# The last chunks of a down-projection, written by hand in a half and two quarters of the tokens

## The chip, the core and the metric

The kernel runs on one core of a Trainium2 chip. The core has a matrix engine (TensorE, PE in the profile, with its weight loads as a row of their own, PEld), a vector engine (DVE), a scalar engine (ACT), a general engine (POOL) and a queue that issues transfers (SP). Each engine works through its own instructions in order and waits on semaphores for the others. The metric is the device time of one execution in microseconds (us); lower is better.

## The reference, cut to what matters

A trunk of two layers over 512 tokens of 1024 channels, all in float32. Only the end of the second layer and the final normalization bear on the change:

```
def swiglu(h, w_gate, w_up, w_down):
    g = jnp.einsum("bsd,df->bsf", h, w_gate)
    u = jnp.einsum("bsd,df->bsf", h, w_up)
    return jnp.einsum("bsf,fd->bsd", jax.nn.silu(g) * u, w_down)
...
        x = x + swiglu(h, w_gate[l], w_up[l], w_down[l])
    return rmsnorm(x, final_norm_g)
```

The final normalization of a token needs the sum of the squares of all its 1024 channels, and so every product of the down-projection for that token. Tokens do not need one another here.

## The kernel before, in words

Activations are kept with channels on the 128 partitions and the 512 tokens along the free dimension: `x[0]` to `x[7]` are eight tiles of 128 channels by 512 tokens. A weight block is 128 by 128. To keep float32 precision each operand is split into a high and a low part in TensorE's float32r type, and a block costs three products: high by high, high by low and low by high (lines 844 to 846 for the stretch in question, 186 to 188 elsewhere). Each product loads its own weights. The low parts of the weights are made by DVE (line 144) from a copy by ACT (line 135), five pairs ahead of their use.

The last down-projection of the second layer is `last_down`. The SwiGLU values come in two halves of 11 blocks of 128 hidden channels; this function handles the second half. For two of the eight output chunks it runs all 11 blocks at once, for the other six only the first 7; this leaves for those six chunks the last 4 blocks (`KL = 4`), whose weights it has put aside in `last`. So the end of the kernel is six chunks of 4 blocks of three products: 72 products over all tokens. They are run once for tokens 0 to 255 and once for tokens 256 to 511, so 144 products of 256 columns.

After each chunk's 12 products, DVE adds the result to `x` (line 848), ACT squares the sum (line 850), and DVE adds the square to a running sum `run` (line 852). After the six chunks of a half, `scale_of` does the normalization: four products of one column each (line 303; float32, so each stands twice in a trace) sum the squares over the partitions, a chain of nine small DVE steps (`rsqrt`, lines 285 to 293) takes the inverse root, two DVE steps build a diagonal matrix (line 315, tile `dg`), and a product (line 330, tile `rbc`) spreads the result over the partitions. Then each chunk of the half, already multiplied by its channel gain on ACT (line 862, tile `fo`), is multiplied by `rbc` on DVE (line 866) or by a copy `rf` of it on POOL (line 864), and pairs of chunks are sent to memory, 256 KB each, four transfers a half (line 868).

What sets the order of all this before the change is a scheduler that reorders instructions within each engine by its own estimate of times. It has laid the first half's normalization under the second half's products, and two of the last products ahead of the end of the 7-block part.

Of the kernel before, what the change touches and what calls it, by code (L numbers as in the profile page):

```python
# [19 lines left out]
F32 = mybir.dt.float32  # L20
F32R = mybir.dt.float32r
I32 = mybir.dt.int32
AF = mybir.ActivationFunctionType
# [5 lines left out]
S = 512  # L29
L = 2  # L30
P = 128
KC = D // P
FF = 2816
FC = FF // P
FH = FC // 2
# [3 lines left out]
RMS_EPS = 1e-6  # L39
# [3 lines left out]
RQ = 0.375 * -0.5  # L43
UNITS = 96
KL = 4
FIN_POOL = [[0, 1, 2, 3, 4], [0, 1]]


C_MIXG, C_FFNG, C_SC, C_GLUB, C_DW, C_DWB, C_LNG, C_LNB, C_SUB = 0, 8, 16, 22, 26, 88, 90, 92, 94
# [29 lines left out]
def trunk(ctx, tc, xT, pos, wu, cv, lamv, cst, out):  # L79
    nc = tc.nc  # L80
    V, A, G, T = nc.vector, nc.scalar, nc.gpsimd, nc.tensor

    def pool(name, bufs, **kw):
        return ctx.enter_context(tc.tile_pool(name=name, bufs=bufs, **kw))
    cp = pool("cp", 1)
    pw = pool("pw", 6)
    ph = pool("ph", 8)
# [15 lines left out]
    x = [cp.tile([P, S], F32, name=f"x{k}") for k in range(KC)]  # L103
# [79 lines left out]
    def mm3(ps, rh, first, last, w=None):  # L183

        hi, lo = w or block()
        T.matmul(ps, lhsT=hi, rhs=rh[:, 0, :], start=first, stop=False)  # L186
        T.matmul(ps, lhsT=hi, rhs=rh[:, 1, :], start=False, stop=False)  # L187
        T.matmul(ps, lhsT=lo, rhs=rh[:, 0, :], start=False, stop=last)  # L188
# [86 lines left out]
        (V if (k == KC - 1 if last is None else last) else eng).tensor_add(run, run, sq)  # L275
        return run

    def rsqrt(a, n, key):

        y = sm.tile([P, n], F32, tag=f"rq{key}", name=f"rq{key}", bufs=2)
        t = sm.tile([P, n], F32, tag=f"rt{key}", name=f"rt{key}", bufs=2)
        a2 = sm.tile([P, n], F32, tag=f"ra{key}", name=f"ra{key}", bufs=2)
        V.tensor_scalar(y.bitcast(I32), a.bitcast(I32), -0.5, 1597463007.0, ALU.mult, ALU.add)
        V.tensor_scalar(a2, a, 0.375 ** 2, None, ALU.mult)
        V.tensor_mul(t, a, y)
        V.tensor_mul(t, t, y)
        V.scalar_tensor_tensor(t, t, -10.0 / 3.0, t, ALU.add, ALU.mult)
        V.scalar_tensor_tensor(y, t, 5.0, y, ALU.add, ALU.mult)  # L290
        V.tensor_mul(t, a2, y)
        V.tensor_mul(t, t, y)
        V.scalar_tensor_tensor(y, t, -3.0, y, ALU.add, ALU.mult)
        return y

    def scale_of(parts, mul, eps, key, pool, ptag, n=4):

        ps = pool.tile([P, n], F32, tag=ptag, name="ssps")  # L300
        for b in range(n):
            for i, t in enumerate(parts):
                T.matmul(ps[:, b:b + 1], lhsT=t[:, b * P:b * P + P], rhs=consts["ones_d"][:, 0:1],
                         start=i == 0, stop=i == len(parts) - 1)
        a = sm.tile([P, n], F32, tag="sca" + key, name="sca", bufs=2)
        V.tensor_scalar(a, ps, mul, eps, ALU.mult, ALU.add)
        y = rsqrt(a, n, key)
# [155 lines left out]
    class Pair:  # L463
# [349 lines left out]
    def last_down(acts):  # L813

        NA = KC - 6
        H = S // 2
        run = pt.tile([P, S], F32, tag="t", name="run")
        for dc in range(KC):  # L820
            n = FH if dc < NA else FH - KL
            ps = acc.tile([P, S], F32, tag="acc", name="od")
            for k in range(n):
                mm3(ps, acts[k], k == 0, k == n - 1)
            V.tensor_add(x[dc], x[dc], ps)
            if dc == 0:
# [6 lines left out]
        outs = [ph.tile([P, 2, S], F32, tag="h", name=f"fo{i}") for i in range(KC // 2)]  # L833
        g = [cvt[:, C_FING + k:C_FING + k + 1] for k in range(KC)]
        rb = []
        for i in range(2):
            cs = slice(i * H, i * H + H)
            for j in range(6):
                p, tag = ((acc, "acc"), (sc, "sc"))[j % 2]
                q = p.tile([P, H], F32, tag=tag, name="ol")  # L840
                for k in range(KL):
                    hi, lo = last[j][k]
                    rh = acts[FH - KL + k]
                    T.matmul(q, lhsT=hi, rhs=rh[:, 0, cs], start=k == 0, stop=False)
                    T.matmul(q, lhsT=hi, rhs=rh[:, 1, cs], start=False, stop=False)
                    T.matmul(q, lhsT=lo, rhs=rh[:, 0, cs], start=False, stop=k == KL - 1)
                t = x[NA + j][:, cs]
                V.tensor_add(t, t, q)
                sq = pe.tile([P, H], F32, tag="e", name="sqh")
                A.activation(sq, t, AF.Square)  # L850
                if j < 5:
                    V.tensor_add(run[:, cs], run[:, cs], sq)
            st = scale_of([run[:, cs], sq], 1.0, RMS_EPS, f"f{i}", tp, "tp", n=2)
            next(st)
            rb.append(next(st))
        for i in range(2):
            cs = slice(i * H, i * H + H)
            r = pt.tile([P, H], F32, tag="t", name="rf")
            A.copy(r, rb[i])
            for k in range(KC):  # L860
                o = outs[k // 2][:, k % 2, cs]
                A.activation(o, x[k][:, cs], AF.Copy, scale=g[k])
                if k in FIN_POOL[i]:
                    G.tensor_mul(o, o, r)
                else:
                    V.tensor_mul(o, o, rb[i])
                if k % 2:
                    nc.sync.dma_start(out[k - 1:k + 1, :, cs].rearrange("k p t -> p k t"), outs[k // 2][:, :, cs])

    def lambdas():  # L870

# [21 lines left out]
    run = None  # L893
    h = []
    state = {}
    for l in range(L):
        cb = l * C_LAYER
        st = {"run": None, "h": [None] * KC}
# [22 lines left out]
        for half in range(2):  # L921
            acts = []
            for f in range(FH):
                if r is None:
                    mr = make_r(run2)
                    next(mr)
                    r = next(mr)
# [4 lines left out]
                t = pt.tile([P, S], F32, tag="t", name="tg")  # L932
# [3 lines left out]
                a = (py if f < 8 else pv).tile([P, 2, S], F32R, tag=("yb", "ya", "v")[f // 4], name="act")  # L936
# [8 lines left out]
        h = st["h"]  # L945
        run = st["run"]
# [109 lines left out]
```

## Time and profile before

| what | value |
| --- | --- |
| median of 3 runs | 1180.51 us (1180.06 to 1187.22) |
| profiled execution | 1177.73 us |
| its span, first to last instruction | 1176.0 us |
| TensorE busy | 1139.2 us, 97% of the span |
| VectorE busy | 642.5 us, 55% |
| mean granted TensorE clock | 0.986 of full speed |

The profiled execution is a run of its own, 2.8 us under the median of the timed ones. Times within it, such as "at 1161.23", are us from the start of its span. In the rows further down, L846 is line 846 of the kernel, `out<-in` are the program's names for tiles, and `xN` counts instructions. The granted clock is 1.00 at 2.4 GHz and 0.50 at 1.2 GHz.

### The profile page before, as it was taken

To read this page: it belongs to the slowest core of one execution; us is meant where nothing else is said; L and a number is where in the kernel's file an instruction comes from. 1 tells how busy PE (TensorE), PEld (TensorE's weight loads), DVE (VectorE), ACT (ScalarE), POOL (GpSimd) and SP (SyncE) were. 2 spreads that over 40 slices of the span, in tenths; PEclk is the share of its full clock that TensorE was granted. 3 is DMA by queue.
4 is the path that set the end of the run, shared out by engine and by line. 5 is a ranking of instruction groups with operands and counts; after the bars stand their busy time and mean duration, and the time that the engine had idled before them with its cause. 6 is when DMAs were issued, how large, how long until landed. Compare 5 with 4: busy or idle time off the path is not lost.

```text
span 1176.0 us, 14329 instructions
## 1 busy us (share of the span) xinstructions
PE 1139.2 (97%) x5238; PEld 944.2 (80%) x5238; DVE 642.5 (55%) x1152; ACT 497.6 (42%) x1023; POOL 187.5 (16%) x217
## 2 busy tenths in 40 slices
PE   7989899999999999999999999999999999999995
PEld 5878787888888888888888787788888888888885
DVE  6687785564443344444436988746544333444345
ACT  6636566643332233333345466665333222333323
POOL 1421212311110010110123212122101000011001
PEclk9999899999999999999999999999999999999998
DMA  5895834432322223232247866453232322323212
GB/s 196 218 219 123 198 85 111 106 125 90 108 90 99 98 91 107 90 102 95 91 130 182 199 147 152 114 134 118 93 104 90 107 91 95 103 90 108 90 55 72
DMA packets 48614, 138.53 MB, mean 118 GB/s; under 512 B 6912, under 2 KB 9216, under 8 KB 48544
## 3 DMA queue, kind: packets, MB, share of 16 engines
q1 hardware_dynamic: 29888, 88.79, 23.5%
q0 software_dynamic: 18656, 48.83, 17.6%
q8 instruction: 41, 0.67, 0.2%
q14 instruction: 29, 0.24, 0.1%
HBM read 122.79 MB, written 2.23 MB: 106 GB/s over the span
## 4 chain that ended last, share of the span: by engine, by line
PE 83%; DVE 6%; DMA 3%; issue 3%; ACT 3%; SPq 1%; POOL 0%; DVEq 0%; ACTq 0%; POOLq 0%
PE od L186 8%; PE od L187 8%; PE od L188 8%; PE gp L188 7%; PE gp L187 7%; PE up L188 7%; PE up L187 7%; PE up L186 7%; PE gp L186 7%; PE qk L186 3%; PE qk L187 2%; PE qk L188 2%; DMA w<-wu 1%; DVE acc L576 1%; PE cc L187 1%
## 5 line engine op out<-in xcount | busy, mean ns | idle before, releaser
L135 ACT CAST w<-raw 128x512 fp32r<-128x512 f32 x384 | 237.6, 622 | 491.8 <-PE od L188 147.1
L144 DVE TENSOR_TENSOR w<-raw,w 128x512 fp32r<-128x512 f32 x265 | 186.8, 706 | 247.2 <-ACT w L135 246.6
L935 POOL TENSOR_TENSOR tg<-tg,r 128x512 f32<-128x512 f32 x44 | 57.7, 1313 | 520.6 <-ACT tg L934 511.0
L187 PE MATMUL gp<-h,w 128*128 128x512 f32 x352 | 137.3, 390 | 0.3 <-DVE h L265 0.3
L188 PE MATMUL gp<-h,w 128*128 128x512 f32 x352 | 137.3, 390 | 0.0
L186 PE MATMUL up<-h,w 128*128 128x512 f32 x352 | 137.2, 390 | 0.0
L186 PE MATMUL gp<-h,w 128*128 128x512 f32 x352 | 137.2, 390 | 0.0
L188 PE MATMUL up<-h,w 128*128 128x512 f32 x352 | 137.1, 390 | 0.0
L187 PE MATMUL up<-h,w 128*128 128x512 f32 x352 | 137.1, 390 | 0.0
L187 PE MATMUL od<-act,w 128*128 128x512 f32 x328 | 127.8, 390 | 0.0
L186 PE MATMUL od<-act,w 128*128 128x512 f32 x328 | 127.8, 389 | 0.0
L188 PE MATMUL od<-act,w 128*128 128x512 f32 x328 | 127.7, 389 | 0.0
L138 POOL DMA_DIRECT2D w<-wu x70 | 60.7, 871 | 282.5 <-ACT w L137 236.8
L576 DVE SCALAR_TENSOR_TENSOR acc<-pad,cvt,acc 128x511 f32<-128x511 f32 (+14 forms) x120 | 88.1, 734 | 2.7
L187 PEld LDWEIGHTS gp<-h,w 128*128 128x128 f32 x352 | 66.1, 188 | 14.5 <-DVE h L265 0.7
L186 PEld LDWEIGHTS up<-h,w 128*128 128x128 f32 x352 | 66.1, 188 | 14.0 <-DVE x L901 0.4
L186 PEld LDWEIGHTS gp<-h,w 128*128 128x128 f32 x352 | 66.1, 188 | 13.8 <-ACT h L264 0.2
L187 PEld LDWEIGHTS up<-h,w 128*128 128x128 f32 x352 | 66.1, 188 | 13.7
L188 PEld LDWEIGHTS up<-h,w 128*128 128x128 f32 x352 | 66.1, 188 | 13.6
L188 PEld LDWEIGHTS gp<-h,w 128*128 128x128 f32 x352 | 66.1, 188 | 13.5
L186 PEld LDWEIGHTS od<-act,w 128*128 128x128 f32 x328 | 61.6, 188 | 12.8
L187 PEld LDWEIGHTS od<-act,w 128*128 128x128 f32 x328 | 61.6, 188 | 12.7
(254 smaller groups left out, 1988.6 us busy)
## 6 DMA issues: line engine op xcount, KB each, us to landing
raw<-wu SPq DMA_DIRECT2D x135, 512.0 KB, 3.4
raw<-wu POOLq DMA_DIRECT2D x56, 512.0 KB, 6.3
w<-wu POOLq DMA_DIRECT2D x70, 256.0 KB, 4.7
pk<-hl SPq DMA_DIRECT2D x64, 128.0 KB, 6.9
pq<-hl SPq DMA_DIRECT2D x64, 64.0 KB, 5.0
x<-xT SPq DMA_DIRECT2D x8, 256.0 KB, 8.2
yT<-fo SPq DMA_DIRECT2D x8, 256.0 KB, 2.2
raw<-wu SPq DMA_DIRECT2D x2, 256.0 KB, 6.7
```

The source lines that it names most:

```text
L135: A.copy(t[:, 0, :], raw)
L138: G.dma_start(t[:, 1, :], wu[u, :, 4 * P * half:4 * P * half + 4 * P], accum_op=ALU.add)
L144: sub()
L186: T.matmul(ps, lhsT=hi, rhs=rh[:, 0, :], start=first, stop=False)
L187: T.matmul(ps, lhsT=hi, rhs=rh[:, 1, :], start=False, stop=False)
L188: T.matmul(ps, lhsT=lo, rhs=rh[:, 0, :], start=False, stop=last)
L576: V.scalar_tensor_tensor(a[:, d:], pad[:, :S - d], cvt[:, c - d:c - d + 1], a[:, d:], ALU.mult, ALU.add)
L935: G.tensor_mul(t, t, r)
```

## The change

The six chunks are run in three parts instead of two: tokens 0 to 255, 256 to 383 and 384 to 511, so 72 products of 256 columns and 144 of 128 columns. The whole end is taken out of the scheduler's hands (`tc.manual_schedule()`), so it stands in each engine's queue as it is written. The sums and the inverse root of a part are written under the next part's products: its sums after the next part's second chunk, the small DVE steps of its root between that part's additions (`between`). Chunks 2 and 3 of the six, and 5 and 6, get the two banks of one PSUM buffer. A chunk pair of the first half is now multiplied in one POOL instruction (512 columns), four of them, and the quarters by DVE, four chunks in one instruction. The multiplications and transfers of both quarters stand at the very end. The output still leaves in eight transfers of 256 KB, but those of the quarters are made of rows of 128 tokens, 512 bytes each, where a half has rows of 1024 bytes.

```
-    def rsqrt(a, n, key):
+    def rsqrt(a, n, key, between=lambda: None):
...
         V.tensor_mul(t, a, y)
+        between()
         V.tensor_mul(t, t, y)
         V.scalar_tensor_tensor(t, t, -10.0 / 3.0, t, ALU.add, ALU.mult)
+        between()
         V.scalar_tensor_tensor(y, t, 5.0, y, ALU.add, ALU.mult)
         V.tensor_mul(t, a2, y)
+        between()
...
+        with tc.manual_schedule():
+            finale(acts, last, run)
+
+    def finale(acts, last, run):
+        NA = KC - 6
+        H = S // 2
+        parts = [slice(0, H), slice(H, H + P), slice(H + P, S)]
...
+        def between(n=1):
+            while todo and n:
+                todo.pop(0)()
+                n -= 1
+
+        def product(j, i):
+            cs = parts[i]
+            n = cs.stop - cs.start
+            if j % 3 == 0:
+                q = acc.tile([P, n], F32, tag="acc", name="ol")
+            else:
+                if j % 3 == 1:
+                    two.append(sc.tile([P, 2, S], F32, tag="sc", name="ol"))
+                q = two[-1][:, j % 3 - 1, :n]
+            for k in range(KL):
+                hi, lo = last[j][k]
+                rh = acts[FH - KL + k]
+                T.matmul(q, lhsT=hi, rhs=rh[:, 0, cs], start=k == 0, stop=False)
+                T.matmul(q, lhsT=hi, rhs=rh[:, 1, cs], start=False, stop=False)
+                T.matmul(q, lhsT=lo, rhs=rh[:, 0, cs], start=False, stop=k == KL - 1)
+            return q
...
+        def step(j, i, sqs):
+            q = product(j, i)
+            cs = parts[i]
+
+            def added():
                 t = x[NA + j][:, cs]
                 V.tensor_add(t, t, q)
+                sq = pe.tile([P, cs.stop - cs.start], F32, tag="e", name="sqh")
                 A.activation(sq, t, AF.Square)
+                sqs[j] = sq
+                if i:
+                    scaled(NA + j, i - 1)
                 if j < 5:
+                    todo.insert(0, lambda: V.tensor_add(run[:, cs], run[:, cs], sq))
+            todo.append(added)
+
+        def wide(o, dst, r, eng):
+            eng.tensor_mul(o, o, r.unsqueeze(1).to_broadcast(list(o.shape)))
+            nc.sync.dma_start(dst.rearrange("k p t -> p k t"), o)
...
+        for j in range(6):
+            step(j, 0, sqs[0])
+            between(2)
+        between(9)
...
+        for i, pool, tag in ((1, tp, "tp"), (2, av, "av")):
+            for j in range(2):
+                step(j, i, sqs[i])
+                between(2)
+            st = scale(i - 1, pool, tag)
+            for j in range(2, 6):
+                step(j, i, sqs[i])
             next(st)
+            between(99)
+            rb = next(st)
+            rbs.append(rb)
+            if i == 1:
+                r = pt.tile([P, H], F32, tag="t", name="rf")
+                A.copy(r, rb)
+                for k in range(4):
+                    leave(k, r, G)
+        st = scale(2, tp, "tp")
+        for j in range(6):
+            scaled(NA + j, 2)
+        next(st)
+        rb = next(st)
+        leave4(0, 1, rbs[1])
+        leave4(4, 1, rbs[1])
+        leave4(0, 2, rb)
+        leave4(4, 2, rb)
```

Up to the end of the 7-block part every engine's queue holds the same work in the same order as before, but for the two early products and the gain multiplications of the two finished chunks. In the rows below `w_8866`, `w_8883`, `w_8900`, `w_8915`, `w_8932` and `w_8948` are the weights of chunks 1 to 6, `x_103` to `x_108` the six tiles of `x`, and the names in brackets are the engines that an instruction waits for.

TensorE, in the second part, where the sums of the first half (`ssps`) stand. Before, second half's chunks 2 and 3:

```order
L846 MATMUL ol<-act,w_8883 128x256
L303 MATMUL ssps<-ones_d,run 128x1 [waits DVE_49,Pool_49]
L844 MATMUL ol<-act,w_8883 128x256
L845 MATMUL ol<-act,w_8883 128x256
L846 MATMUL ol<-act,w_8883 128x256
L844 MATMUL ol<-act,w_8900 128x256
L845 MATMUL ol<-act,w_8900 128x256
```

Now, first quarter's chunks 2 and 3:

```order
L875 MATMUL ol<-act,w_8883 128x128
L301 MATMUL ssps<-ones_d,run 128x1 [waits DVE_49,Pool_49]
L301 MATMUL ssps<-ones_d,sqh 128x1 [waits Activation_49]
L301 MATMUL ssps<-ones_d,run 128x1
L301 MATMUL ssps<-ones_d,sqh 128x1
L873 MATMUL ol<-act,w_8900 128x128 [waits DVE_49]
L874 MATMUL ol<-act,w_8900 128x128
```

The sums stand in one block, the products around them have 128 columns in place of 256, and chunk 3 begins with a wait for DVE.

TensorE, in the first half, from chunk 2 to the next chunk. Before (the scheduler ran chunk 4 next):

```order
L844 MATMUL ol<-act,w_8883 128x256
L845 MATMUL ol<-act,w_8883 128x256
L846 MATMUL ol<-act,w_8883 128x256
L844 MATMUL ol<-act,w_8915 128x256 [waits Activation_49]
L845 MATMUL ol<-act,w_8915 128x256
```

Now:

```order
L873 MATMUL ol<-act,w_8883 128x256
L874 MATMUL ol<-act,w_8883 128x256
L875 MATMUL ol<-act,w_8883 128x256
L873 MATMUL ol<-act,w_8900 128x256 [waits DVE_49,Activation_49]
L874 MATMUL ol<-act,w_8900 128x256
```

Chunk 3 writes the second bank of the buffer that chunk 2 has just filled, and its wait on DVE runs up to the addition that reads chunk 2. The same stands between chunks 5 and 6.

DVE, from the end of the last products on. Before:

```order
L848 TENSOR_TENSOR x_107<-x_107,ol 128x256 [waits PE_49]
L852 TENSOR_TENSOR run<-run,sqh 128x256 [waits Activation_49]
L848 TENSOR_TENSOR x_108<-x_108,ol 128x256 [waits PE_49]
L866 TENSOR_TENSOR fo_8953<-fo_8953,rbc 128x256 [waits Activation_49]
L866 TENSOR_TENSOR fo_8954<-fo_8954,rbc 128x256 x2
L306 TENSOR_SCALAR sca<-ssps 128x2 [waits PE_49]
```

Now:

```order
L889 TENSOR_TENSOR x_107<-x_107,ol 128x128 [waits PE_49]
L896 TENSOR_TENSOR run<-run,sqh 128x128 [waits Activation_49]
L889 TENSOR_TENSOR x_108<-x_108,ol 128x128
L313 TENSOR_SCALAR sca<-ssps 128x1 [waits PE_49]
...
L322 TENSOR_SCALAR dg<-idr,sca 128x128 [waits DVE_49]
L900 TENSOR_TENSOR fp_8957<-fp_8957,rbc 128x512
L900 TENSOR_TENSOR fp_8957<-fp_8957,rbc 128x512 [waits Activation_49]
L900 TENSOR_TENSOR fp_8958<-fp_8958,rbc 128x512 [waits PE_49,Activation_49]
L900 TENSOR_TENSOR fp_8958<-fp_8958,rbc 128x512 [waits Activation_49]
```

The three multiplications ahead of the root are gone, the addition of chunk 6 has no wait of its own (that of chunk 5 now waits for the last product of both), and four wide multiplications close the queue.

## Rows read from the trace of the kernel before

**Rows 1.** The page: its span, and busy time of each engine.
```profile
span 1176.0 us, 14329 instructions
PE 1139.2 (97%) x5238; PEld 944.2 (80%) x5238; DVE 642.5 (55%) x1152; ACT 497.6 (42%) x1023; POOL 187.5 (16%) x217
```

**Rows 2.** Chain of waits, last 15 us: start, length, what.
```profile
1161.39 0.12 PE ol L846
...
1162.39 1.09 DVE fo L866 x3
...
1163.53 1.07 PE ssps L303 x8
...
1164.81 0.42 DVE rqf L285
...
1165.30 0.61 DVE rtf L287
...
1167.32 0.49 DVE dg L315 x2
...
1167.94 1.21 PE rbc L330 x2
...
1170.00 0.33 DVEq L1052
1170.33 1.32 DVE fo L866 x4
```

**Rows 3.** Timeline of TensorE, first and last of the 256-column products: start, length, what.
```profile
1143.20 0.39 PE L188 MATMUL od<-act,w 128*128 128x512 f32 x1
...
1143.43 0.28 PE L846 MATMUL ol<-act,w 128*128 128x256 f32 x1
...
1161.23 0.28 PE L846 MATMUL ol<-act,w 128*128 128x256 f32 x1
```

**Rows 4.** The same view around 30 us: products of one column.
```profile
29.79 1.02 PE L303 MATMUL ssps<-ones_d,run 128*128 128x1 f32 x8 [2.46 <-issue]
30.67 0.47 PE L186 MATMUL cc<-h,w 128*128 128x512 f32 x1
```

**Rows 5.** The same view at 84 us: products of 128 columns.
```profile
84.31 0.41 PE L483 MATMUL ps<-maskr,idr 128*128 128x128 f32 x1
84.53 0.41 PE L481 MATMUL ps<-pk,pq 128*128 128x128 f32 x1
```

**Rows 6.** Groups by line and shape: busy us, mean ns | idle before.
```profile
L844 PE MATMUL ol<-act,w 128*128 128x256 f32 x47 | 13.4, 287 | 0.0
...
L848 DVE TENSOR_TENSOR x<-x,ol 128x256 f32<-128x256 f32 x12 | 5.1, 421 | 2.9 <-PE ol L846 2.6
...
L315 DVE TENSOR_SCALAR dg<-idr,sca 128x128 f32<-128x128 f32 x4 | 1.0, 285 | 0.1
...
L525 ACT ACTIVATE junk<-o 128x128 bf16<-128x128 f32 x32 | 8.9, 277 | 6.4 <-PE o L523 6.4
...
L933 DVE TENSOR_TENSOR tg<-gp,r 128x512 f32<-128x512 f32 x44 | 30.2, 691 | 52.5 <-PE gp L188 52.5
...
L935 POOL TENSOR_TENSOR tg<-tg,r 128x512 f32<-128x512 f32 x44 | 57.7, 1313 | 520.6 <-ACT tg L934 511.0
```

**Rows 7.** Stretches: length, busy of PE, PEld, DVE, ACT, POOL, clock, DMA, GB/s.
```profile
27.00:30.60 3.60, 1.14 (x10) 0.84 (x8) 2.56 (x4) 1.96 (x4) 2.53 (x6) 1.00 0.72 202
30.60:34.00 3.40, 3.40 (x17) 2.81 (x18) 2.81 (x18) 0.77 (x3) 1.63 (x4) 1.00 0.95 213
80.30:83.70 3.40, 1.14 (x5) 0.57 (x4) 3.26 (x5) 2.22 (x5) 0.78 (x1) 1.00 1.09 265
83.70:87.10 3.40, 3.27 (x11) 2.89 (x12) 3.29 (x6) 1.23 (x3) 0.62 (x2) 0.51 1.06 275
```

**Rows 8.** DMA queue, 27.15 to 28.35, then 1169.5 to 1175.5: packets, MB, share of 16.
```profile
q1 hardware_dynamic: 160, 0.07, 26.1%
...
q1 hardware_dynamic: 1088, 1.05, 52.1%
```

More of the change, by code (lines that the diff above doesn't have):

```diff
@@ L45 @@
 KL = 4
-FIN_POOL = [[0, 1, 2, 3, 4], [0, 1]]
 C_MIXG, C_FFNG, C_SC, C_GLUB, C_DW, C_DWB, C_LNG, C_LNB, C_SUB = 0, 8, 16, 22, 26, 88, 90, 92, 94
@@ L294, in rsqrt, with sums @@
         return y
-    def scale_of(parts, mul, eps, key, pool, ptag, n=4):
-        ps = pool.tile([P, n], F32, tag=ptag, name="ssps")
+    def sums(ps, parts, n):
         for b in range(n):
@@ L304, in scale_of @@
                          start=i == 0, stop=i == len(parts) - 1)
+    def scale_of(parts, mul, eps, key, pool, ptag, n=4, between=lambda: None):
+        ps = parts
+        if isinstance(parts, list):
+            ps = pool.tile([P, n], F32, tag=ptag, name="ssps")
+            sums(ps, parts, n)
         a = sm.tile([P, n], F32, tag="sca" + key, name="sca", bufs=2)
         V.tensor_scalar(a, ps, mul, eps, ALU.mult, ALU.add)
-        y = rsqrt(a, n, key)
+        y = rsqrt(a, n, key, between)
         def diag(p, v, dt, tag, eng, **kw):
@@ L832, in last_down @@
         last = [[block() for _ in range(KL)] for _ in range(6)]
-        outs = [ph.tile([P, 2, S], F32, tag="h", name=f"fo{i}") for i in range(KC // 2)]
-        g = [cvt[:, C_FING + k:C_FING + k + 1] for k in range(KC)]
[L835 to L846, printed above, removed]
+        with tc.manual_schedule():
+            finale(acts, last, run)
@@ new lines, in finale, with scaled @@
+    def finale(acts, last, run):
+        NA = KC - 6
+        H = S // 2
+        parts = [slice(0, H), slice(H, H + P), slice(H + P, S)]
+        g = [cvt[:, C_FING + k:C_FING + k + 1] for k in range(KC)]
+        half = [ph.tile([P, 2, H], F32, tag="h", name=f"fo{i}") for i in range(KC // 2)]
+        quarter = [ph.tile([P, KC, P], F32, tag="h", name=f"fp{i}") for i in range(2)]
+        todo = []
+        two = []
+        def between(n=1):
[18 more added lines that the diff above has]
+            return q
+        def scaled(k, i):
+            o = quarter[i - 1][:, k, :] if i else half[k // 2][:, k % 2, :]
+            A.activation(o, x[k][:, parts[i]], AF.Copy, scale=g[k])
+        def step(j, i, sqs):
+            q = product(j, i)
+            cs = parts[i]
+            def added():
@@ L847, in last_down @@
                 t = x[NA + j][:, cs]
                 V.tensor_add(t, t, q)
-                sq = pe.tile([P, H], F32, tag="e", name="sqh")
+                sq = pe.tile([P, cs.stop - cs.start], F32, tag="e", name="sqh")
                 A.activation(sq, t, AF.Square)
+                sqs[j] = sq
+                if i:
+                    scaled(NA + j, i - 1)
                 if j < 5:
-                    V.tensor_add(run[:, cs], run[:, cs], sq)
-            st = scale_of([run[:, cs], sq], 1.0, RMS_EPS, f"f{i}", tp, "tp", n=2)
@@ L854, in last_down @@
-            next(st)
[L855 to L868, printed above, removed]
+                    todo.insert(0, lambda: V.tensor_add(run[:, cs], run[:, cs], sq))
@@ new lines, in step, with leave, leave4 @@
+            todo.append(added)
+        def wide(o, dst, r, eng):
+            eng.tensor_mul(o, o, r.unsqueeze(1).to_broadcast(list(o.shape)))
+            nc.sync.dma_start(dst.rearrange("k p t -> p k t"), o)
+        def leave(k, r, eng):
+            wide(half[k], out[2 * k:2 * k + 2, :, parts[0]], r, eng)
+        def leave4(k, i, r):
+            wide(quarter[i - 1][:, k:k + 4, :], out[k:k + 4, :, parts[i]], r, V)
+        for i in range(3):
+            for k in range(NA):
+                scaled(k, i)
@@ new lines, in finale, with scale @@
+        sqs = [{}, {}, {}]
+        for j in range(6):
+            step(j, 0, sqs[0])
+            between(2)
+        between(9)
+        def scale(i, pool, tag):
+            n = (parts[i].stop - parts[i].start) // P
+            ps = pool.tile([P, n], F32, tag=tag, name="ssps")
+            sums(ps, [run[:, parts[i]], sqs[i][5]], n)
+            return scale_of(ps, 1.0, RMS_EPS, f"f{i}", pool, tag, n=n, between=between)
+        rbs = []
+        for i, pool, tag in ((1, tp, "tp"), (2, av, "av")):
[5 more added lines that the diff above has]
+                step(j, i, sqs[i])
+            next(st)
+            between(99)
[6 more added lines that the diff above has]
+                    leave(k, r, G)
```

## The prediction, made before the changed kernel ran

> **What bounds the kernel now.** First the page: TensorE is busy for 1139.2 of the 1176.0 us, so the kernel is a chain of products with little between them [rows 1], and all that the change touches lies at its end. Then the chain of waits for the last 15 us, where TensorE stops being the bound: the last product ends at 1161.5, and from there on small steps follow one another on DVE, TensorE and ACT until the last multiplication ends at 1171.65 [rows 2]. Behind it lie 4.35 us to the end of the span, in which the last transfers land and the engines meet. Then TensorE's timeline for the products of the six chunks [rows 3], and the groups of this stretch, which say whether they wait for anything: they do not, the idle time before them is 0.0 [rows 6].
>
> So there are two stretches to price. In the first, TensorE alone counts: what makes its products dearer, or makes it wait, is paid in full. In the second nothing runs beside the normalization of the last 256 tokens: what is taken out of it is gained in full.
>
> **The first stretch.** A product of 256 columns follows the one before it after 0.12 us: two starts lie 0.12 apart in the chain and in the timeline, and 144 of them with the eight one-column sums of the first half laid between them fill 18.2 us, from the end of the 7-block part at 1143.43 (two of the 144 ran ahead of it) to 1161.35, a pitch behind the last start [rows 3]. The change keeps 72 of these products, 72 x 0.12 = 8.6 us, and turns the other 72 into 144 of 128 columns. Work in columns is the same, the number of weight loads doubles.
>
> The price of a 128-column product decides the forecast. Below it is bounded by the columns alone: 512 columns take 0.23 and 256 take 0.12 [rows 3], so half of that again would be about 0.065. Above it is bounded by 0.12, the 256-column pitch. The nearest row in kind is a product that has almost no columns but loads 128 by 128 weights like all others: eight of one column start at 29.79, and the next product stands at 30.67, so each takes 0.11 [rows 4]. A product is thus not repeated faster than 0.11 us however few columns it has. The 128-column products of the attention agree: they stand 0.22 apart [rows 5] in a stretch where the granted clock is 0.51 [rows 7], which is 0.11 at full clock. I take 0.11: 144 x 0.11 = 15.8 us. The page "TensorE: Matmul & The Clock Gate" of the Trainium skill, section "Back-to-back issue gap", gives about 81 ns for each product of 128 columns in a stream of loads and products; the rows differ, with 110 ns even for one column. By the page the 144 would take 11.7 us and the sum below would be 4.1 us lower.
>
> Also on TensorE: the sums of the first two parts, 8 and 4 instructions at 0.11, 1.3 us; the spreading product of the first half, which moves in among the products, two instructions at 0.12, 0.24 us. And new waits: in the first half chunk 3 waits until the addition of chunk 2 has read their common buffer, and chunk 6 for chunk 5. That is the end of the product behind its pitch, 0.28 - 0.12 = 0.16 [rows 3], an addition of 0.42 [rows 6] and two hand-overs of 0.05 (such a one lies between 1163.48 and 1163.53 [rows 2]): 0.68 each, 1.4 for both. Queued behind the wait is all of TensorE's work. In the quarters the same wait stands behind the sums; these cover it in the first (0.88 us) and all but some 0.1 in the second; I take nothing for both, at most 0.3 each. The first stretch so takes 8.6 + 15.8 + 1.3 + 0.24 + 1.4 = 27.4 us against 18.2: **9.2 us more**.
>
> What hides under it: the roots of the first two parts, about 2.5 us of small DVE steps each, under the products of four chunks, 5.3 us; POOL's four multiplications at 1.31 us [rows 6], 5.3 us, and their transfers, under the second quarter's products, 7.9 us; the extra gain multiplications on ACT between its squares, six of them under the last root. DVE's additions, now 18 for 12, each 0.29 for 128 columns (the diagonal's step of that size [rows 6]), with 1.3 us of products per chunk above them. If POOL's cover were gone its transfers would join the last ones; there are about 10 us to spare (7.9 + 7.35 - 5.3).
>
> **The second stretch, after the last product.** Before, it is 1171.65 - 1161.35 = 10.3 us. Now, step by step:
> - To the sums. The additions of chunks 5 and 6 both wait for chunk 6's last product, so they come one after the other: rest of the product 0.15, addition 0.29, square 0.28 (ACT on 128 columns [rows 6]), addition to the running sum 0.29, addition 0.29, square 0.28, two sum instructions 0.36, five hand-overs of 0.05: 2.2 us. Before, the sums end at 1164.60 [rows 2], 3.25 us behind the last product, with the three multiplications of the first half (1.09) ahead of them.
> - The root, to the end of the diagonal. Before 1164.62 to 1167.81, 3.2 us; in it two steps of 0.42 and 0.61 [rows 2] where their neighbours take 0.17. I take these two as of the usual length, 0.7 less (else up to 0.7 more), and one diagonal step for two, 0.24 less: 2.25 us.
> - The multiplications. Before, the spreading product (1.21), a copy (0.38) and six of them follow, 3.85 us. Now four of 512 columns at 0.69 [rows 6], of which the first two belong to the first quarter and run while the last spreading product does; starts lie 0.05 closer than the ends, as three take 1.09 for 3 x 0.42 before. With the 0.33 of fetching instructions that stands in the chain [rows 2] this is 2.9 us.
>
> Together 7.35 us: **3.0 us less**. The queue of SP holds nothing else there.
>
> **The last transfers.** Both kernels send the last 1.05 MB in four transfers at the end, so the 4.35 us behind the last multiplication stay, but the rows are of 512 bytes now. In 1169.5 to 1175.5 the 16 engines spent 52.1% of 6 us, 50 engine-us, on 1.05 MB of 1024-byte rows; in 27.15 to 28.35, where 512-byte rows run among other traffic, 26.1% of 1.2 us, 5.0 engine-us, on 0.07 MB [rows 8]. Per byte that is 1.5 times as much, and 3.1 us of transfer would become 4.7. Bounds: nothing to 1.6 us. The rows of the right size are the nearer ones, but they were not alone; I take 0.8.
>
> **Sum.** 9.2 - 3.0 + 0.8 = 7.0 us more. The profiled execution of 1177.7 would become 1184.7; as it stands 2.8 under the median of the timed runs, the median of 1180.5 becomes **1187.5**, 0.6% slower. That is inside 1%, 11.8 us, about what a measurement of this kernel can tell from no change.
>
> **The rivals.**
> 1. *The clock falls to 1.2 GHz in the quarters* (slower). Place: TensorE between the first half and the last product. Price: a 128-column product takes 0.22 there [rows 5], 0.11 more. It decides by 1% when (11.8 - 7.0) / 0.11 = 44 or more products of the 144 lie behind the fall; with 72 behind it the time is 1195.4, with all 1203.3. For it: the clock fell at 83.7, after a stretch in which TensorE was busy for 1.14 of 3.4 us, and was 0.51 in the next, which held 128-column products [rows 7]; the quarter products keep moving columns for about half of their pitch, and the trace has no stretch at full clock made of such products alone. Against it: with 1.14 of 3.6 us and a gap of 2.46 [rows 4] the clock stayed at 1.00 [rows 7], and the change puts no gap over 0.7 us into the products.
> 2. *Weight loads hide under 128 columns.* The pitch is then 0.065 and 6.5 us fall away; some 1.8 come back, since chunk 3 of each quarter then waits for chunk 2's addition and the roots for less cover: 7.0 - 4.7 = 2.3, so 1182.8. For it only the columns [rows 3], against it the one-column rows [rows 4]. The page's 81 ns, by the trace not borne out, would give 1183.4.
> 3. *The order pays as drawn.* Loads hide, nothing waits, 512-byte rows cost nothing: 9.2 - 1.4 - 6.5 - 3.0 = -1.7, 1178.8. It needs three unlikely things at once.
>
> That the change would not do what it says can be left out: the order of the queues shows it done.
>
> **How the numbers follow.** Forecast 0.70, with 1184 to 1191 for its own bounds (the transfers, the two long steps, the waits in the quarters, a pitch of 0.12); rival 1 0.14 (1192 to 1203), rival 2 0.12 (1182 to 1184), rival 3 0.04. The range 1181.5 to 1194 leaves out rival 3 and most of rival 1, and has room for the 7 us by which the three runs before differ. Faster by over 1% is out of reach even if the whole 10.3 us were gained: 0.02. Slower by over 1% is rival 1 and a little of the forecast's upper end: 0.16. Within 1%: 0.82.
>
> **What would show it.** In the profile after: 128-column products 0.11 apart over some 17 us at clock 1.00; two idle times of about 0.7 on TensorE in the first half, released by DVE; the last product at about 1170.6; the last multiplication at about 1178; four transfers behind it. A pitch near 0.07 makes rival 2 right, a clock of 0.50 before the last product rival 1. The prediction is wrong if the last product stands before 1168, or if the stretch behind it is not 2 to 4 us shorter.

## The result, and the profile after

| | before | after |
| --- | --- | --- |
| median | 1180.28 us, 4 runs (1177.84 to 1187.22) | 1195.68 us, 4 runs (1192.8 to 1206.08) |
| ratio, with its 95% interval | | 1.0151 (1.0103 to 1.0200) |
| profiled execution | 1177.73 us, span 1176.0 | 1197.12 us, span 1195.3 |
| mean granted TensorE clock | 0.986 | 0.974 |

The change makes the kernel 1.5% slower. The forecast was 0.6%, 1187.5 us, with a range up to 1194; the median lies above it, where rival 1 stands. In the profiled executions the difference is 1195.3 - 1176.0 = 19.3 us. The page of the changed kernel answers to [rows 1]:

```profile
span 1195.3 us, 14513 instructions
PE 1159.9 (97%) x5312; PEld 964.0 (81%) x5312; DVE 645.0 (54%) x1169; ACT 500.3 (42%) x1036; POOL 188.0 (16%) x214
```

TensorE has 74 instructions more and is busy 20.7 us longer (1159.9 against 1139.2). So nearly all of the loss is TensorE at work, not TensorE waiting. Next, its timeline from the end of the 7-block part to the last product (start, length, what; in brackets an idle time and who ended it), which answers to [rows 3]. Lines 873 to 875 are the three products of a block, and a product's pitch is the distance of two starts:

```profile
1143.00 0.39 PE L187 MATMUL od<-act,w 128*128 128x512 f32 x1
1143.23 0.28 PE L873 MATMUL ol<-act,w 128*128 128x256 f32 x1
...
1146.87 0.36 PE L873 MATMUL ol<-act,w 128*128 128x256 f32 x1 [0.60 <-DVE x L889]
...
1152.02 0.36 PE L873 MATMUL ol<-act,w 128*128 128x256 f32 x1 [0.60 <-DVE x L889]
...
1157.39 0.27 PE L873 MATMUL ol<-act,w 128*128 128x128 f32 x1
1157.50 0.27 PE L874 MATMUL ol<-act,w 128*128 128x128 f32 x1
1157.61 0.33 PE L875 MATMUL ol<-act,w 128*128 128x128 f32 x1
1157.73 0.42 PE L873 MATMUL ol<-act,w 128*128 128x128 f32 x1
1157.95 0.41 PE L874 MATMUL ol<-act,w 128*128 128x128 f32 x1
...
1183.55 0.41 PE L875 MATMUL ol<-act,w 128*128 128x128 f32 x1
1183.76 0.73 PE L337 MATMUL rbc<-dg,ones_d 128*128 128x128 f32 x2
```

The two waits of the first half are there. Then 128-column products stand 0.11 apart, and from 1157.73 to the last one 0.21 apart, with a spreading product and two sums among them and without a gap. The same stretch in a table (from:to, length, busy time of PE, PEld, DVE, ACT and POOL with their instructions, granted clock, DMA, GB/s) gives the reason:

```profile
1143.23:1150.00 6.77, 6.17 (x51) 5.99 (x50) 3.88 (x8) 1.87 (x4) 0.00 (x0) 1.00 0.00 0
1150.00:1157.61 7.61, 7.00 (x61) 6.83 (x61) 3.47 (x12) 2.67 (x7) 0.00 (x0) 1.00 0.01 2
1157.61:1170.00 12.39, 12.39 (x59) 12.21 (x58) 3.43 (x19) 3.09 (x9) 0.77 (x1) 0.50 0.00 0
1170.00:1183.76 13.76, 13.76 (x66) 13.76 (x66) 4.75 (x20) 2.41 (x8) 4.24 (x4) 0.50 0.23 77
1183.76:1195.30 11.54, 2.71 (x9) 1.94 (x9) 5.07 (x19) 2.95 (x10) 0.00 (x0) 0.50 0.32 92
```

The clock column falls from 1.00 (2.4 GHz) to 0.50 (1.2 GHz) at 1157.6 and stays there to the end. TensorE is busy for all 12.39 us of the next line and all 13.76 of the one after: it loses the clock while it never stops. What it did before was 30 of the 128-column products, with four sums between them; its last idle time before the fall ended at 1152.02, 5.6 us earlier.

Last, the chain of waits behind the last product (start, length, what), which answers to [rows 2], and the DMA queue from 1189 to 1195 (packets, MB, share of 16 engines), which answers to [rows 8]:

```profile
1184.00 0.30 DVE x L889
...
1184.32 0.32 ACT sqh L891
...
1184.67 0.30 DVE run L896
...
1185.01 0.59 PE ssps L301 x2
...
1185.61 0.60 PE ssps L301 x2
...
1186.64 0.14 DVE rtf L286
...
1188.16 0.29 DVE dg L322
1188.45 0.91 DVE fp L900 x2
...
1189.48 0.76 DVEq L1131
1190.24 0.60 DVE fp L900
```

```profile
q1 hardware_dynamic: 2112, 1.05, 62.0%
```

From 1183.76 to the end of the last multiplication, 1190.84, it is 7.1 us, where before took 10.3. Every small step of the root takes 0.14 to 0.17 here. From there to the end of the span it is 4.46 us (before 4.35).

### The profile page after: what moved, and what is told of

Its sections match the earlier page's. It is cut to its first block, busy times and chain, and to the rows that moved or that the text cites. A ratio compares the mean times of both kernels' runs of the same rounds, so it can differ in the third digit from the quotient of the medians.

```text
span 1195.3 us, 14513 instructions
## 1 busy us (share of the span) xinstructions
PE 1159.9 (97%) x5312; PEld 964.0 (81%) x5312; DVE 645.0 (54%) x1169; ACT 500.3 (42%) x1036; POOL 188.0 (16%) x214
## 4 chain that ended last, share of the span: by engine, by line
PE 82%; DVE 6%; DMA 4%; issue 3%; ACT 3%; SPq 1%; POOL 0%; DVEq 0%; ACTq 0%; POOLq 0%
PE od L185 8%; PE od L187 7%; PE od L186 7%; PE up L187 7%; PE up L186 7%; PE gp L186 7%; PE gp L187 7%; PE up L185 7%; PE gp L185 6%; PE qk L185 2%; PE qk L187 2%; PE qk L186 2%; DMA raw<-wu 2%; PE cc L185 1%; PE cc L186 1%
```

## The experiments

What made the clock fall? **T1**: the 128-column products themselves. **T2**: what stands before and among them up to the fall, the two waits of 0.60 us and the block of one-column sums. **T3**: the order by hand as such.

One thing has to be known for reading the traces. The work up to the end of the 7-block part is the same in all kernels here, but in the profiled executions it ends anywhere between 1137.3 and 1150.5 us; before alone ranges from 1171.88 to 1187.88 in 29 runs of one batch. So the traces are compared from the last product of the 7-block part on, and all times of that kind are in one table at the end of this section.

**1. Two halves in the order by hand.** The quarters are undone, the shared buffers and their two waits stay.

```diff
-        parts = [slice(0, H), slice(H, H + P), slice(H + P, S)]
+        parts = [slice(0, H), slice(H, S)]
...
-        leave4(0, 1, rbs[1])
-        leave4(4, 1, rbs[1])
-        leave4(0, 2, rb)
-        leave4(4, 2, rb)
+        for k in range(4):
+            leave(k, 1, rb, V)
```

> Undoes the quarters alone: two halves again (144 products of 256 columns), in the order written by hand, with the shared PSUM buffers and their two waits. Theory (narrow products make the clock fall): granted clock 1.00 to the last product; first stretch 18.2 of before + 0.24 + 1.2 of waits = 19.6 us, stretch behind the last product about 8.5 instead of 10.3; span within 1 us of 1176.0, ratio to before 1.00. Rival (the two waits make the clock fall): the waits are here too, so the clock falls in the second half, 50 to 70 products at 0.22 instead of 0.12, span 1181 to 1184. Rival (the hand order itself is what costs): about as slow as the change, ratio over 1.01.

Measured: 1182.38 us, ratio 1.0028 (1.0003 to 1.0053). The stretch from the first product after the 7-block part to the last one, and the one behind it:

```profile
1143.90:1163.70 19.80, 18.59 (x153) 18.22 (x152) 10.98 (x34) 6.39 (x15) 0.00 (x0) 1.00 0.00 1
1163.70:1181.00 17.30, 3.03 (x14) 1.76 (x12) 9.61 (x20) 4.29 (x11) 4.93 (x4) 0.67 0.36 121
```

With the same waits, the same block of sums and the same order but 256 columns the clock holds to the last product (mean clocks of 0.982 to 0.989 in all ten runs). T2 and T3 fall as causes by themselves. The total that was expected with T1 is missed all the same: the stretch behind the last product is 17.3 us where before has 14.7 (1161.35 to 1176.0). The timeline of that stretch (start, length, engine, what) shows a thing that has nothing to do with the clock:

```profile
1166.83 4.93 POOL L899 TENSOR_TENSOR fo<-fo,rf 128x512 f32<-128x512 f32 x4 [48.55 <-ACT rf L932]
...
1167.21 0.91 DVE L284 TENSOR_SCALAR rqf<-sca 128x2 int32<-128x2 int32 x1
...
1168.16 1.18 DVE L286 TENSOR_TENSOR rtf<-sca,rqf 128x2 f32<-128x2 f32 x1
1169.37 1.19 DVE L288 TENSOR_TENSOR rtf<-rtf,rqf 128x2 f32<-128x2 f32 x1
1170.59 1.19 DVE L289 SCALAR_TENSOR_TENSOR rtf<-rtf 128x2 f32<-128x2 f32 x1
1171.81 0.16 DVE L291 SCALAR_TENSOR_TENSOR rqf<-rtf,rqf 128x2 f32<-128x2 f32 x1
```

Three steps of two elements per partition take 1.2 us each, and one takes 0.9, as long as POOL's four multiplications run, 1166.83 to 1171.76; 1.2 us is about as long as one of these (4.93 / 4). From then on such a step takes 0.16. Experiments 8 and 9 come back to it.

**2. The quarters, with 256 columns streamed.** Each product of a quarter streams the 256 columns of both quarters, and half of what it makes is not used.

```diff
-            cs = parts[i]
+            cs = parts[i] if i == 0 else slice(H, S)
...
-            return q
+            return q[:, parts[i].start - cs.start:parts[i].stop - cs.start]
```

> The change as it is, but each quarter's products stream 256 columns (both quarters of the second half), of which only the quarter's own 128 are used. Twice the columns, same number of products and weight loads, same order and waits. Theory (narrow products make the clock fall): clock 1.00 to the last product, 144 x 0.12 = 17.3 us for the quarters, first stretch 28.7 us, 10.5 more than before, less 3.0 behind it: span about 1183.7, ratio 1.006, so FASTER than the change by some 10 us although it streams twice the columns. Rival (the waits or the block of one-column sums make it fall): the clock falls as in the change, span 1194 to 1198.

Measured: 1188.91 us, ratio 1.0078 (1.0052 to 1.0104), mean clocks 0.983 to 0.989 in all six runs.

```profile
1142.70:1152.00 9.30, 8.09 (x65) 7.70 (x65) 5.22 (x12) 2.71 (x6) 0.00 (x0) 1.00 0.00 0
1152.00:1162.00 10.00, 10.00 (x87) 10.00 (x86) 4.79 (x23) 3.25 (x9) 0.00 (x0) 1.00 0.01 2
1162.00:1172.60 10.60, 10.22 (x85) 10.08 (x84) 7.11 (x23) 4.09 (x13) 5.13 (x4) 1.00 0.30 100
```

Same instructions, same order, same waits as the change; only the columns of 144 products are doubled. The clock holds, and the kernel is faster by some 7 us than the change for computing more (ratios of 1.0078 and 1.0151; in the profiled executions the stretch from the 7-block part to the end is 41.4 us against 52.3). T1 forecast it.

**3. A PSUM buffer for each chunk.** The waits are taken away by what makes them, the common buffer.

```diff
-            if j % 3 == 0:
-                q = acc.tile([P, n], F32, tag="acc", name="ol")
-            else:
-                if j % 3 == 1:
-                    two.append(sc.tile([P, 2, S], F32, tag="sc", name="ol"))
-                q = two[-1][:, j % 3 - 1, :n]
+            p, tag = ((acc, "acc"), (sc, "sc"))[j % 2]
+            q = p.tile([P, n], F32, tag=tag, name="ol")
```

> The change with a PSUM buffer of its own for each chunk in the first half and quarters as before the change (alternating two pools), which takes the two waits of 0.6 us out of the first half. Theory (narrow products): the clock still falls in the first quarter; 1.2 us less than the change if it falls at the same product, span 1192 to 1196. Rival (the waits make the clock fall): clock 1.00 to the last product, span about 1181.

Measured: ten runs in two groups. Four take 1176.5 to 1181.4 us at mean clocks of 0.986 to 0.991, six take 1192.2 to 1199.8 at 0.970 to 0.979. (The ratio, 1.006, 1.0013 to 1.0107, is taken from eight of the ten and mixes both, so it prices neither.) The profiled execution is one of the four:

```profile
1146.00:1155.00 9.00, 9.00 (x83) 9.00 (x82) 5.27 (x25) 3.94 (x11) 0.00 (x0) 1.00 0.01 2
1155.00:1164.10 9.10, 9.10 (x82) 9.05 (x81) 5.75 (x22) 3.61 (x13) 5.10 (x4) 1.00 0.35 117
1164.10:1174.70 10.60, 1.89 (x9) 1.24 (x8) 4.79 (x18) 2.74 (x10) 0.00 (x0) 0.60 0.36 100
```

This is what the forecast described, but for the two waits: all 144 narrow products at clock 1.00, 0.11 apart. No trace of one of the six was kept. Their times and mean clocks lie where those of the change do, so without the waits the clock most likely still falls in most executions; but it can also hold.

**4. The half and the quarters left to the scheduler.** Before, with the three parts of the change and nothing else of it.

```diff
-        for i in range(2):
-            cs = slice(i * H, i * H + H)
+        parts = [slice(0, H), slice(H, H + P), slice(H + P, S)]
+        for i in range(3):
+            cs = parts[i]
```

> The kernel before with the same half and two quarters, but left to the scheduler, with its own PSUM buffers and the multiplications as before. Theory (narrow products): the clock falls here too, span 1190 to 1198, ratio 1.01 to 1.02. Rivals (waits, or the hand order, are what costs): clock stays, span 1178 to 1185.

Measured: 1178.41, 1179.94, 1198.28 and 1202.15 us, at mean clocks of 0.989, 0.990, 0.972 and 0.968. Two groups again, without any order by hand. That the clock fell in the narrow products of the two slower ones is read from their times and mean clocks alone, for want of a trace; if so, the choice of narrow parts is what costs, whoever sets the order. That the order by hand is no cause by itself is shown by experiment 1. With the clock held (the profiled execution) the products take as long as in experiment 3:

```profile
1138.80:1165.00 26.20, 26.20 (x230) 26.15 (x228) 16.29 (x62) 12.43 (x36) 3.61 (x5) 1.00 0.12 41
```

**5. The change again**, for the spread of its executions; no edit.

> The change as it is, for the spread of its executions. Every trace is measured from the last product of the 7-block part to the end of the span: before 32.8 us, the change 52.3, the change with a PSUM buffer for each chunk 37.4 in its profiled execution, in which the clock stayed at 1.00 to the last product, though its other executions reach from 1177 to 1200. T1 (narrow products alone make the clock fall, in some executions and not in others): some executions of this one keep it too, at a mean clock of 0.985 or more and about 6 us (37.4 + 1.2 of waits - 32.8) above before, 1182 to 1186. T2 (the two waits of 0.6 us in front of them decide): none does, all stay at 0.98 or lower and above 1191.

Measured: 1196.13 us, ratio 1.0148 (1.0110 to 1.0186), six runs at mean clocks of 0.974 to 0.979. By the times and mean clocks, and by the two traces kept, the clock fell in ten of ten executions, with the four of the result. T1 had expected some to keep it, and that was wrong. In the trace kept it fell after 40 narrow products, in that of the result after 30. With a buffer for each chunk four of ten kept the clock; if the waits did nothing, all four would fall to that side by chance once in some 23 times. That is a hint that the waits make the fall surer, and no proof. By experiment 3 they are not needed for it, and where the columns are wide they don't cause one.

**6. Both: a buffer for each chunk and 256 columns.** Experiment 3 with the edit of experiment 2.

> A PSUM buffer for each chunk, and the quarters' products stream 256 columns instead of 128 (half of the columns are thrown away). With this all four combinations of narrow or wide and waits or none are there. T1: the clock stays at 1.00 to the last product in all executions, and the time is before plus 7 us (41.4 of the wide one less its 1.6 of waits, against 32.8): 1.006. T2 says the same, since there are no waits. A rival, T3, that the order by hand itself loses the clock: falls here too, 1.012 or more.

Measured: 1186.26 us, ratio 1.0048 (1.0016 to 1.0079), mean clocks 0.983 to 0.993 in twelve runs. All of the products at clock 1.00:

```profile
1150.30:1178.00 27.70, 27.70 (x231) 27.61 (x231) 16.45 (x58) 10.17 (x29) 5.15 (x4) 1.00 0.12 39
```

That closes the square. By their times and mean clocks (three of the runs have a trace) the clock fell with narrow products in 16 of 20 runs of the order by hand, 10 of 10 with the waits and 6 of 10 without; with wide ones no run of 18 has the low mean clock (6 with, 12 without).

**7. Three quarters of the tokens, then one.** 72 products of 384 columns and 72 of 128, from experiment 3.

```diff
-        parts = [slice(0, H), slice(H, H + P), slice(H + P, S)]
+        M = S - P
+        parts = [slice(0, M), slice(M, S)]
...
+            for k in range(2):
+                leave(k, r, G)
+            between(99)
+            step(5, i, sqs[i])
+            leave(2, rb, V)
+            between(99)
+            leave(3, rb, V)
```

> Three quarters of the tokens and then one, in the order by hand, a PSUM buffer for each chunk: 72 products of 384 columns and 72 of 128, the first part's spreading product after the fifth chunk of the second, its multiplications shared by POOL and DVE. With the clock held: 72 x 0.17 + 72 x 0.11 + 1.5 for sums and spreading = 21.7 for the products, to the sums 2.2, root 2.3, two multiplications 1.3, transfers 4.4: 31.9 us against 32.8, so before less 1, ratio 0.999. T1: the clock still falls in some executions, but with at most 72 narrow products behind it, so at most 7.9 us more; the falls cost half of what they cost the change or less. If only the waits counted (T2), it falls in none.

Measured: 1183.24 us, ratio 1.0031 (1.0004 to 1.0059). In the profiled execution there is no wait on TensorE before the last product, and the clock falls within the narrow ones. Its table of stretches, then its timeline from the last of its sums to the fall:

```profile
1150.70:1163.50 12.80, 12.80 (x76) 12.76 (x76) 6.95 (x13) 3.25 (x6) 0.00 (x0) 1.00 0.01 1
1163.50:1169.70 6.20, 6.20 (x56) 6.20 (x56) 2.93 (x14) 2.71 (x7) 0.00 (x0) 0.97 0.00 0
1169.70:1176.80 7.10, 7.10 (x31) 6.46 (x30) 3.70 (x13) 2.27 (x6) 1.70 (x1) 0.50 0.00 0
```

```profile
1166.97 0.36 PE L301 MATMUL ssps<-ones_d,sqh 128*128 128x1 f32 x2
...
1169.12 0.27 PE L872 MATMUL ol<-act,w 128*128 128x128 f32 x1
1169.23 0.28 PE L870 MATMUL ol<-act,w 128*128 128x128 f32 x1
...
1169.72 0.42 PE L870 MATMUL ol<-act,w 128*128 128x128 f32 x1
1169.93 0.41 PE L871 MATMUL ol<-act,w 128*128 128x128 f32 x1
```

A fall without any wait, after 43 narrow products: the waits are not needed, and now a trace shows it. The block of sums is not tested by this. Six sums stand among the narrow products here too, the last of them in the first line of the timeline; four stand there in both traces of the change, and also in those of experiments 3 and 4, where the clock held. Fewer narrow products lie behind it, and the loss is a fifth of the change's. How many of the twelve runs fell can't be read from their mean clocks (0.978 to 0.989, before 0.979 to 0.990), since a fall this late moves the mean too little.

**8. Two halves by hand, a buffer for each chunk, POOL one chunk earlier.** From experiment 1.

```diff
-            for j in range(2, 6):
+            for j in range(2, 5):
                 step(j, i, sqs[i])
             next(st)
-            between(99)
             rb = next(st)
...
+            between(99)
+            for k in range(3):
+                leave(k, 0, r, G)
+            step(5, i, sqs[i])
+            between(99)
+            leave(3, 0, r, G)
```

> Two halves in the order by hand with a PSUM buffer for each chunk, and the first half's spreading product and POOL's four multiplications one chunk earlier than in the halves before. There, the root behind the last product took 4.9 us instead of 2.3: four of its DVE steps took about 1.2 us each while POOL's multiplications of 512 columns ran beside them. If POOL's instructions lengthen the DVE steps, those of the root that start after POOL is done take 0.17 again, and the stretch from the 7-block part to the end shrinks from 37.3 by 1.2 (waits) and some 2 to 4 us: 32 to 34, ratio 0.998 to 1.001. If instead the clock of 1.2 GHz behind the last product lengthens them, they stay at 1.2 us: 36, ratio 1.003. The clock stays at 1.00 to the last product by all theories but T3.

Measured: 1180.05 us, ratio 1.0015 (0.9984 to 1.0045). Its timeline:

```profile
1166.49 5.14 POOL L895 TENSOR_TENSOR fo<-fo,rf 128x512 f32<-128x512 f32 x4 [43.96 <-ACT rf L925]
...
1170.47 1.18 DVE L286 TENSOR_TENSOR rtf<-sca,rqf 128x2 f32<-128x2 f32 x1
1171.68 0.16 DVE L288 TENSOR_TENSOR rtf<-rtf,rqf 128x2 f32<-128x2 f32 x1
```

POOL is done at 1171.63; the step that begins before takes 1.18, those behind it 0.16. These run at a clock of 0.50 (1171.6 to 1173), so TensorE's low clock is not what lengthens such steps. The end shrinks from 37.3 to 33.3 us, as forecast (0.7 of it ahead of the last product, where the waits are gone): POOL's instructions lengthen DVE's steps.

**9. Two halves by hand, with all of that cleared up.** From experiment 8: the first half's sums one chunk earlier, its spreading product after the fourth chunk, three multiplications on POOL from there, one on DVE, and the last four shared.

```diff
-            for j in range(2):
-                step(j, i, sqs[i])
-                between(2)
-            st = scale(i - 1, pool, tag)
-            for j in range(2, 5):
-                step(j, i, sqs[i])
+        step(0, 1, sqs[1])
+        between(2)
+        st = scale(0, tp, "tp")
+        for j in range(1, 4):
+            step(j, 1, sqs[1])
...
+        leave(3, 0, rb, V)
...
+        leave(0, 1, r, G)
+        for k in range(1, 4):
+            leave(k, 1, rb, V)
```

> Two halves in the order by hand, a PSUM buffer for each chunk, everything of the first half's normalization moved forward under the second half's products (its sums after the first chunk, its spreading product after the fourth, three of its multiplications on POOL from then on, the fourth on DVE behind the last addition), and the last four multiplications shared, one on POOL and three on DVE. From the last product of the 7-block part to the end of the span: products 144 x 0.12 with 1.5 for the sums and the spreading laid between them, 18.8; to the sums 2.2 to 3; root 2.5, its steps at 0.17 now, since POOL is done before it starts; spreading 1.2; multiplications 2.3; transfers 4.4: 31.4 to 32.2 against 32.8 of before, ratio 0.999. If POOL's instructions do not lengthen DVE's steps but something else does, the root stays at 3.9 to 4.9 and the stretch at 33 to 35. By T1 the clock stays at 1.00 to the last product in all executions.

Measured: 1179.2 us, ratio 0.9993 (0.9958 to 1.0027). Its timeline:

```profile
1164.05 1.26 POOL L895 TENSOR_TENSOR fo<-fo,rf 128x512 f32<-128x512 f32 x1 [0.17 <-ACT fo L875]
...
1168.23 0.16 DVE L286 TENSOR_TENSOR rtf<-sca,rqf 128x2 f32<-128x2 f32 x1
```

POOL is done at 1165.31, and every step of the root takes 0.16. The end as a whole is 34.7 us and not 31.4 to 32.2: the sums end 4.4 us after the last product instead of 2.2 to 3 (a running-sum addition takes 1.30 us beside POOL, what is queued behind it on DVE comes late, and the sums themselves run at the fallen clock), and 5.05 us lie behind the last multiplication. It has the lowest ratio of the orders by hand, some 1.5% under the change's, and can't be told from before.

All traces, each from the start of the last product of the 7-block part:

| kernel | columns in the quarters | waits | to the last product, us | to the end of the span, us |
| --- | --- | --- | --- | --- |
| before | (halves) 256 | no | 18.0 | 32.8 |
| the change | 128 | yes | 40.6 | 52.3 |
| the change again (5) | 128 | yes | 39.5 | 51.3 |
| 3, clock held | 128 | no | 26.6 | 37.4 |
| 4, clock held | 128 | no | 26.3 | 38.1 |
| 2 | 256 | yes | 30.0 | 41.4 |
| 6 | 256 | no | 27.8 | 38.6 |
| 7, clock fell late | 384, then 128 | no | 26.0 | 37.8 |
| 1 | (halves) 256 | yes | 19.9 | 37.3 |
| 8 | (halves) 256 | no | 19.2 | 33.3 |
| 9 | (halves) 256 | no | 19.0 | 34.7 |

## Why the prediction was wrong

**The step that failed** is the price of the narrow products: "I take 0.11: 144 x 0.11 = 15.8 us". The 0.11 is right at clock 1.00, in the change up to 1157.61 and in experiment 3 for all 144. But 114 of the 144 stand behind the fall, 0.21 apart. From 1157.61 to 1183.76 it is 26.2 us; at full clock 115 products, one spreading product and two sums (four instructions) would be 115 x 0.112 + 0.3 + 0.44 = 13.6. So 12.5 of the 13.1 us by which the first stretch missed (40.5 from 1143.23 to 1183.76, forecast 27.4) are the clock.

**Rival 1 named this** and priced it per product; with the 114 that the trace shows it is 7.0 + 114 x 0.11 = 19.5 us, and the traces differ by 19.3. That they agree to 0.2 is partly luck: the first stretch is longer by 0.6 than this sum has it, the transfers cheaper by 0.7. What was wrong was its chance, 0.14. The argument against it was that the clock had stayed at 1.00 across a gap of 2.46 us, and that the change puts in no gap over 0.7: it took idleness for what the clock goes by. The trace before could not settle it. Its stretch of 83.7 to 87.1, with TensorE busy for 3.27 of 3.4 us and 128-column products in it, has a clock of 0.51 [rows 7], but the clock fell there before the first of them began, behind an idle time (a mean of 0.51 over 3.4 us leaves less than 0.1 us at 1.00):

```profile
83.83 0.47 PE L481 MATMUL ps<-pk,pq 128*128 128x128 f32 x1 [2.39 <-ACT vt L459]
```

And that trace has no more than some ten products of 128 columns or fewer in a row anywhere. That the quarters would run at full clock was an assumption without a row of its kind, and it was given too high a chance. The page "TensorE: Matmul & The Clock Gate" of the Trainium skill, section "What's actually happening", lets the clock go by how busy TensorE has been. By busy time as the profile counts it this would have held the clock at 1.00, and the trace does not agree: 0.50 over 26 us at 100% busy.

**The other terms** stood:
- The pitch of 256-column products, 0.12, and the chance of rival 2: 128 columns at clock 1.00 take 0.11 and not 0.065, and rivals 2 and 3 are out. The 81 ns of the Trainium skill's page that the prediction weighed ("TensorE: Matmul & The Clock Gate", "Back-to-back issue gap") isn't borne out either.
- The two waits: TensorE is idle for 0.60 in each. The forecast of 0.68 was for all that a wait adds to the pitches: the 72 products take 10.3 us (1143.23 to 1153.53) where the pitches alone make 8.6, so it was 0.83 each. In the quarters there are none.
- The stretch behind the last product: 7.1 us, forecast 7.35. Within it the sums end 2.4 us after the last product instead of 2.2, as two of them take 0.6 at the fallen clock; the root takes 2.2 (forecast 2.25), and the multiplications 2.4 (forecast 2.9). Time for fetching instructions was added to the forecast without need: the 0.76 in the chain above lies beside DVE's work, which goes on without idle time from 1188.37 to 1190.84, 2.47 us for four multiplications. The two long steps of before, 0.42 and 0.61 [rows 2], were left out of the forecast as not to be expected, and they are gone.
- The last transfers: 512-byte rows take 62.0% against 52.1% of 6 us, 1.19 times as much per byte and not 1.5; behind the last multiplication that is 0.1 us, forecast 0.8. This was the mis-sized term.

Together, with the clock held, the forecast of +7.0 would have been a little high: experiment 3 has no waits and ends 37.4 - 32.8 = 4.6 us later than before, against 7.0 - 1.4 = 5.6.

**What stays open** is what decides in a single execution whether the clock holds under narrow products (experiments 3 and 4 have both, with the same instructions), and whether the waits, or the sums that stand among the narrow products in every kernel with a fall, add to it.

## What to carry to other kernels

Before a product is cut into narrower ones, ask what keeps the clock up, not only what a product costs at the present clock: here a stretch that was fully busy with narrow products ran at half the clock. Look in the trace before for a stretch of the same kind, as long and as dense, and read its clock column; where there is none, the full clock is an assumption, and its chance has to say so. Where the mean clock of an execution falls in two groups, read each group by itself; a single profiled execution, like that of experiment 3, can show the kind one. Here 3 us of gain after the last product were not worth a doubling of half of the products ahead of it: with the clock held, experiment 3 still ends 4.6 us later than before.

## What the runs showed of the hardware that was not expected

- TensorE loses its clock while it is busy without a gap: 0.50 from 1157.6 on, after 30 products of 128 columns with a weight load each (40 and 43 in the traces of experiments 5 and 7; in those of 3 and 4 it holds for all 144). In the traces kept, 256 and 384 columns with the same loads hold 1.00. Doubling the columns made the kernel faster by some 7 us.
- POOL's multiplications of 512 columns lengthen DVE steps that read two operands from SBUF: a step of 2 elements takes 1.18 to 1.19 us beside them and 0.16 without, a running-sum addition 1.30 (experiment 9) instead of 0.43. DVE's multiplications with one operand in PSUM are not lengthened (three in 1.88 us beside one of POOL's in experiment 9). The page "SBUF — State Buffer" of the Trainium skill, section "Who interferes with whom", has this rule: a VectorE instruction with two SBUF inputs blocks against a GpSimd instruction that reads SBUF, for all of its length. For these steps the traces agree. Of the two long steps of before [rows 2] it fits the second (0.61, two operands): POOL multiplies there from 1162.43 to 1165.88, and the steps from 1165.94 on take 0.17. The first (0.42) reads one operand, so that sentence doesn't cover it, and yet the same step takes 0.91 beside POOL in experiment 1 and 0.17 without it in experiment 9; why is not shown.
- The last transfers in 512-byte rows cost 1.19 times as much per byte as in 1024-byte rows, 62.0% against 52.1% of the same 6 us and 1.05 MB.
